# Layer norm with residual: three early loads moved from SyncE's DMA queue to ScalarE's

## The chip, the cores and the metric

The kernel runs on one core of a Trainium2 chip. The metric is device time in microseconds (us), which includes some 1.3 us outside the profiled span. "Fast" is the undisturbed state (granted clock 1.0).

## The reference

```python
# x, residual: (16, 1024, 512) float32; gamma, beta: 512; eps 1e-5
z = x + residual
mean = np.mean(z, axis=-1, keepdims=True)
var = np.var(z, axis=-1, keepdims=True)
out = (gamma * (z - mean) / np.sqrt(var + eps) + beta).astype(np.float32)
```

That is 33.5 MB of x, 33.5 MB of residual and 33.5 MB of output: 100.7 MB that must cross the DMA engines (100.68 MB in the profile), and little arithmetic.

## The kernel before

A "row" below is one 512-vector in each of the 128 partitions, 0.262 MB; there are 128 rows of x, of residual and of output. `x16+16` in the plan is one DMA that loads rows 16 to 31 of x; `r` is the residual, `o` a store. SyncE issues all of them, in this order:

```python
BLOCK = 16; Z_ROWS = 64; R_ROWS = 32        # rows in the buffers zbuf and rbuf
PLAN = """
x0+8 r0+8 x8+8 r8+8 x16+16 r16+16 x32+16 r32+16
x48+16 r48+16 o0+16 r64+16 x64+16 o16+16 r80+16 x80+16
... o64+16 o80+16 o96+16 o112+12 o124+4
"""
ADDS = [4, 4, 8] * 7 + [4] * 4              # rows of GpSimd's adds, in order
EARLY = 2                                   # the first two loads go ahead of the opening barrier

for k, src in enumerate((gamma, beta)):     # 2 KB each, on ScalarE's queue
    nc.scalar.dma_start(out=gb_row[:, k * D : (k + 1) * D], in_=src[None, :]).then_inc(s_gb[k], 16)
...
def move(out, in_, s):
    i = nc.sync.dma_start(out=out, in_=in_).then_inc(s, 16)
    if len(first) < EARLY:
        first.append(i.ins)                 # moved ahead of the barrier at the end of the build
...
    elif kind == "r":
        wait_rows(s_add, "add", lo + n - R_ROWS)   # rbuf holds 32 rows: r32 waits for 16 added rows
        move(part(rbuf, R_ROWS, lo, n), dram(rf, lo, n), sr[loads_r.index((lo, n))])
```

GpSimd (POOL in the profile) adds x and residual as both land. ScalarE (ACT) makes the sums, VectorE (DVE) normalizes in place, SyncE stores. TensorE spreads gamma and beta over the partitions once, in the opening.

## Time and profile before

| | us |
|---|---|
| median, first 3 runs | 238.73 (238.37 to 238.76) |
| span of the profiled run | 236.9 |
| ACT busy, DVE busy, POOL busy | 185.5, 177.2, 143.0 |

The page of the kernel before: the span in 40 slices of 5.9 us with the busy share of the DMA engines in tenths and the rate, then the DMA queues (packets, MB, share of 16 engines' time), then the chain of work that ended last, by engine.

```profile
DMA  8999999999999999999999999999999999999996
GB/s 310 443 432 426 426 443 443 443 443 443 426 415 398 443 443 443 426 420 409 431 437 443 443 443 432 420 407 429 443 437 437 409 432 448 437 420 437 426 430 285
q1 hardware_dynamic: 4176, 100.67, 99.2%
q10 hardware_dynamic: 4, 0.00, 0.0%
DMA 71%; POOL 9%; ACT 9%; DVE 2%; issue 2%; SPq 1%; ACTq 0%; DVEq 0%; POOLq 0%
```

Queue q1 is SyncE's ring, q10 ScalarE's; a ring is the queue of transfers that one issuing engine hands to the DMA engines. (A slice of the GB/s line counts whole packets of 16 or 32 KB, so it goes in steps of about 5.5, 32 KB in 5.92 us, and can show more than the engines keep up: 443 here, where 16 packets of 32 KB in 1213 ns are 432.) One ring alone keeps all 16 DMA engines busy for 99.2% of the span, in every slice but the two ends. The DMA engines bound this kernel; no compute engine is busy more than 78%.

The timeline of the kernel before, in its opening: start us, length us, engine, line, operation, operands; in brackets what an idle engine waited for. SPq and ACTq are the sequencers of SyncE and ScalarE, issuing DMAs.

```profile
0.00 0.38 SPq L146 DMA_DIRECT2D zbuf<-in_x_dram  x1
0.43 0.42 SPq L146 DMA_DIRECT2D rbuf<-in_residual_dram  x1
1.91 0.33 SPq L146 DMA_DIRECT2D zbuf<-in_x_dram  x1
1.92 0.52 ACTq L124 DMA_DIRECT2D gb_row<-in_gamma_dram  x1
...
12.33 8.95 POOL L180 TENSOR_TENSOR zbuf<-zbuf,rbuf 128x2048 f32<-128x2048 f32 x2 [11.90 <-DMA rbuf<-in_residual_dram]
22.12 8.87 POOL L180 TENSOR_TENSOR zbuf<-zbuf,rbuf 128x4096 f32<-128x4096 f32 x1 [0.83 <-DMA rbuf<-in_residual_dram]
41.55 17.83 POOL L180 TENSOR_TENSOR zbuf<-zbuf,rbuf 128x2048 f32<-128x2048 f32 x3 [10.56 <-DMA rbuf<-in_residual_dram]
...
59.41 0.33 SPq L146 DMA_DIRECT2D rbuf<-in_residual_dram  x1
```

The last line is the issue of r48, which must wait until 32 rows are added (until 59.39 us). By then the ring still holds work until x48 lands at 70.53 us. The packet records of the trace add what the page does not print: the first packets start at 1.01 us, a 16 KB packet takes 611 ns and a 32 KB packet 1213 ns at the median, one after the other on each engine, and the 16 engines are idle for 1.17 us on average up to 20 us and for about 0.06 us in all from there to 220 us. (Idle time here is the mean over 16 engines of the time without a packet of 512 bytes or more.)

### The profile page before, as it was taken

To read this page: it belongs to the slowest core of one execution; us is meant where nothing else is said; L and a number is where in the kernel's file an instruction comes from. 1 tells how busy PE (TensorE), PEld (TensorE's weight loads), DVE (VectorE), ACT (ScalarE), POOL (GpSimd) and SP (SyncE) were. 2 spreads that over 40 slices of the span, in tenths; PEclk is the share of its full clock that TensorE was granted. 3 is DMA by queue.
4 is the path that set the end of the run, shared out by engine and by line. 5 is a ranking of instruction groups with operands and counts; after the bars stand their busy time and mean duration, and the time that the engine had idled before them with its cause. 6 is when DMAs were issued, how large, how long until landed. Compare 5 with 4: busy or idle time off the path is not lost.

```text
span 236.9 us, 1471 instructions
## 1 busy us (share of the span) xinstructions
PE 3.7 (2%) x4; PEld 1.2 (0%) x4; DVE 177.2 (75%) x290; ACT 185.5 (78%) x545; POOL 143.0 (60%) x29
## 2 busy tenths in 40 slices
PE   0600000000000000000000000000000000000000
PEld 0100000000000000000000000000000000000000
DVE  0001977939699999999898989896989895698920
ACT  2019879497999999999999998979998956999300
POOL 0098920999799699604995059944995049950000
DMA  8999999999999999999999999999999999999996
GB/s 310 443 432 426 426 443 443 443 443 443 426 415 398 443 443 443 426 420 409 431 437 443 443 443 432 420 407 429 443 437 437 409 432 448 437 420 437 426 430 285
DMA packets 4181, 100.68 MB, mean 425 GB/s; under 512 B 466, under 2 KB 466, under 8 KB 468
## 3 DMA queue, kind: packets, MB, share of 16 engines
q1 hardware_dynamic: 4176, 100.67, 99.2%
q14 instruction: 1, 0.01, 0.0%
q10 hardware_dynamic: 4, 0.00, 0.0%
HBM read 67.11 MB, written 33.55 MB: 425 GB/s over the span
## 4 chain that ended last, share of the span: by engine, by line
DMA 71%; POOL 9%; ACT 9%; DVE 2%; issue 2%; SPq 1%; ACTq 0%; DVEq 0%; POOLq 0%
DMA out_dram<-zbuf 49%; DMA rbuf<-in_residual_dram 16%; POOL zbuf L180 9%; DMA zbuf<-in_x_dram 6%; ACT junk_s L212 5%; ACT junk_m L202 4%; SPq L146 1%; DVE zbuf L240 1%; DVE zbuf L252 1%; ACTq L202 0%; DVEq L240 0%; ACT std L221 0%; DVE rstd L249 0%; ACTq L193 0%; POOLq L177 0%
## 5 line engine op out<-in xcount | busy, mean ns | idle before, releaser
L180 POOL TENSOR_TENSOR zbuf<-zbuf,rbuf 128x2048 f32<-128x2048 f32 (+1 forms) x25 | 142.8, 5740 | 67.6 <-DMA zbuf<-in_x_dram 40.8
L240 DVE SCALAR_TENSOR_TENSOR zbuf<-zbuf,nm,gamma_p 128x512 f32 x128 | 87.1, 743 | 46.3 <-ACT junk_s L212 46.3
L202 ACT ACTIVATE junk_m<-zbuf 128x512 f32 x128 | 74.9, 585 | 29.1 <-POOL zbuf L180 27.5
L212 ACT ACTIVATE junk_s<-zbuf,nm 128x512 f32 x128 | 88.8, 694 | 1.0
L252 DVE SCALAR_TENSOR_TENSOR zbuf<-zbuf,rstd,beta_p 128x512 f32 x128 | 87.1, 743 | 1.1
L212 ACT ACTIVATION_READ_ACCUMULATOR junk_s<-zbuf,nm 128x1 f32 x128 | 23.9, 187 | 0.0
L202 ACT ACTIVATION_READ_ACCUMULATOR junk_m<-zbuf 128x1 f32 x128 | 23.9, 187 | 0.0
L221 ACT ACTIVATE std<-ssq,eps_t 128x4 f32<-128x4 f32 x32 | 9.5, 297 | 3.0
L249 DVE RECIPROCAL rstd<-std 128x4 f32<-128x4 f32 x32 | 5.5, 170 | 0.0
L190 ACT ACT_TABLE_LOAD x1 | 1.3, 1283 | 2.7 <-PEq L60 2.7
L132 PE MATMUL gamma_p<-gb_row,ones 1*128 1x512 f32 x2 | 2.0, 1119 | 7.2 <-DMA gb_row<-in_gamma_dram 7.2
L132 PE MATMUL beta_p<-gb_row,ones 1*128 1x512 f32 x2 | 1.9, 1052 | 0.0
L127 DVE MEMSET ones<- 1x128 f32 x1 | 0.2, 165 | 2.0 <-PEq L60 2.0
L132 PEld LDWEIGHTS beta_p<-gb_row,ones 1*128 1x128 f32 x2 | 0.7, 328 | 1.0 <-issue 0.5
L132 PEld LDWEIGHTS gamma_p<-gb_row,ones 1*128 1x128 f32 x2 | 0.5, 308 | 7.1 <-issue 7.1
L288 POOL MEMSET const-float32-0.0<- 128x1 f32 x1 | 0.1, 98 | 0.2 <-issue 0.2
L288 POOL MEMSET const-bfloat16-1.0<- 128x1 bf16 x1 | 0.1, 101 | 0.0
L288 POOL MEMSET const-uint8-127<- 128x1 uint8 x1 | 0.1, 101 | 0.0
L288 POOL MEMSET const-float32-1.0<- 128x1 f32 x1 | 0.1, 98 | 0.0
L128 DVE MEMSET eps_t<- 128x1 f32 x1 | 0.1, 59 | 0.0
## 6 DMA issues: line engine op xcount, KB each, us to landing
rbuf<-in_residual_dram SPq DMA_DIRECT2D x7, 4096.0 KB, 30.5
out_dram<-zbuf SPq DMA_DIRECT2D x7, 4096.0 KB, 28.6
zbuf<-in_x_dram SPq DMA_DIRECT2D x5, 4096.0 KB, 28.9
zbuf<-in_x_dram SPq DMA_DIRECT2D x6, 2048.0 KB, 14.9
rbuf<-in_residual_dram SPq DMA_DIRECT2D x2, 2048.0 KB, 15.7
out_dram<-zbuf SPq DMA_DIRECT2D x1, 3072.0 KB, 13.5
out_dram<-zbuf SPq DMA_DIRECT2D x1, 1024.0 KB, 10.2
gb_row<-in_gamma_dram ACTq DMA_DIRECT2D x1, 2.0 KB
```

Source lines behind the costliest of these rows:

```text
L127: nc.vector.memset(ones[:, :], 1.0).then_inc(s_const, 1)
L132: nc.tensor.matmul(dest[:, :], ones[:, :], gb_row[:, k * D : (k + 1) * D], start=True, stop=True).then_inc(s_pe, 1)
L146: i = nc.sync.dma_start(out=out, in_=in_).then_inc(s, 16)
L180: nc.gpsimd.tensor_tensor(out=z, in0=z, in1=part(rbuf, R_ROWS, lo, n), op=ALU.add).then_inc(s_add, n)
L190: act.preload_act_table_set("sqrt_and_others")
L202: i = act.activation(out=junk_m[k][:, :], in_=zk[k], func=ACT.Identity, scale=-inv_d, accum_out=nm[j][:, k : k + 1],)
L212: i = act.activation(out=junk_s[k][:, :], in_=zk[k], func=ACT.Square, bias=nm[j][:, k : k + 1], accum_out=ssq[j][:, k : k + 1],)
L221: act.activation(out=std[j][:, :], in_=ssq[j][:, :], func=ACT.Sqrt, bias=eps_t[:, 0:1], scale=inv_d,).then_inc(s_std, TURN)
L240: dve.scalar_tensor_tensor(out=zk[k], in0=zk[k], scalar=nm[j][:, k : k + 1], in1=gamma_p[:, :], op0=ALU.add, op1=ALU.mult,)
L249: dve.reciprocal(out=rstd[j][:, :], in_=std[j][:, :]).then_inc(s_dve, TURN)
L252: i = dve.scalar_tensor_tensor(out=zk[k], in0=zk[k], scalar=rstd[j][:, k : k + 1], in1=beta_p[:, :], op0=ALU.mult, op1=ALU.add,)
L288: nc = _bacc.Bacc("TRN2", target_bir_lowering=False, num_devices=1)
```

## The change

The intent is that two rings feed the DMA engines in the opening, instead of one sequencer that issues load after load.

```diff
-    def move(out, in_, s):
-        i = nc.sync.dma_start(out=out, in_=in_).then_inc(s, 16)
+    def move(out, in_, s, eng=nc.sync):
+        i = eng.dma_start(out=out, in_=in_).then_inc(s, 16)
 ...
             wait_rows(s_add, "add", lo + n - R_ROWS)
-            move(part(rbuf, R_ROWS, lo, n), dram(rf, lo, n), sr[loads_r.index((lo, n))])
+            eng = nc.scalar if lo + n <= R_ROWS else nc.sync
+            move(part(rbuf, R_ROWS, lo, n), dram(rf, lo, n), sr[loads_r.index((lo, n))], eng)
```

ScalarE now issues r0 ahead of the barrier, then gamma, beta, r8 and r16. SyncE issues x0, x8, x16, x32 and all the rest.

## The prediction

> **What bounds the kernel now.** The DMA engines. The table of DMA queues has q1 (SyncE's ring) busy for 99.2% of 16 engines' span of 236.9 us, for 100.67 MB. A 16 KB packet takes 611 ns at its median, a 32 KB packet 1213 ns, back to back: 16 x 16384 B / 611 ns = 429 GB/s. [...] 100.68 MB at 429 to 432 GB/s is 233 to 235 us (estimate from those packets); 2 to 4 us are left for both ends. ACT is busy 78%.

> **The opening.** In the timeline SyncE issues x0 at 0.00 and r0 at 0.43 us, then x8 to x32 from 1.91 to 4.26 us, 0.33 to 0.49 us each. The first packets start at 1.0 us and take 1.1 to 1.5 us; from 2.3 us the engines never run dry: x0 alone is 8 packets of 611 ns per engine, 4.9 us. A second ring has no gap to fill; 1.0 us before the first packet and some 0.6 us of its latency are idle, but x0's issue, unchanged, sets these.

> **What moves.** r0, r8 and r16 go to ScalarE's queue: r0 before the opening barrier, r8 and r16 behind gamma and beta. ScalarE gets three issues of 0.4 us; its table load (1.28 us, from 2.71 us) comes 0.5 to 1 us later. Its first activation waits for POOL until 17.06 us: free.

> **Order of landing.** [...] No run shows it yet. If it holds, x0 lands near 12 us instead of 7.3, with r0 still near 12.2; x8 and r8 near 22 (were 17.1 and 22.0); x16 and r16 near 41 (were 31.7 and 41.4). Adds need both inputs, so the first, third and fourth start as now (12.33, 22.12, 41.55 us). Gamma and beta fall in behind r0 and land near 12 us instead of 7; PE ends near 15 us, and DVE first needs them at 22.77 us: free. r32 is still issued at 31.0 us behind the third add, r48 at 59.4 us, while the ring's work lasts to 70.5 us (landing of x48): 11 us of slack. Nothing reaches steady state or tail.

> **Time.** Bytes, packet times and ends are unchanged: I predict 238.6 us, 8 in 10 within 237.7 to 240.0. Faster by over 2%: 0.01. Within 2%: 0.95. Slower by over 2%: 0.04.

> **What would show it.** Queues: q1 loses 8.4 MB (32 of 384 rows of 0.26 MB) to q10; their shares still sum to about 99%. x0 and r0 land within 1 us of each other near 12 us; x16 and r16 near 41. POOL's first adds start within 0.5 us of before. PE moves by 5 us; DVE's loop does not. The rate over the span is 424 to 427 GB/s. Wrong if the GB/s of slices 2 to 7 drop, or adds start over 1 us later.

> **What would make it wrong.** (1) Switching rings costs time per packet: 1% of 39 us is 0.4 us, 10% would be 4 us. (2) Engines share unequally: with SyncE's ring favoured, x32 overtakes r16 and delays the fourth add; beyond 11 us the DMA queue runs dry. [...]

Cut where marked: a figure for the DMA rate, a rule for how an engine shares two rings, and a third risk. "It" in "If it holds" is that rule, so the landings there were the author's estimate; what the trace shows of them comes below. The sum: 233 to 235 us for the bytes, from the packet times, and 2 to 4 us for both ends, 235 to 239 in all, and the 238.6 predicted is the measured time before, with nothing added.

## The result, and the profile after

The changed kernel takes 238.62 us at the median (238.19 to 239.56, 6 runs), the kernel before 238.64 us (238.37 to 238.76, 6 runs). Ratios in this document are the mean time of one kernel's fast runs over that of the other's of the same rounds, so not quite the ratio of the medians: here 1.0006, with a 95% interval from 0.9984 to 1.0028.

The page of the changed kernel, the same lines:

```profile
DMA  8999999999999999999999999999999999999995
GB/s 309 438 430 449 435 415 441 435 441 441 430 441 435 369 441 441 435 441 441 424 430 424 419 424 435 441 410 430 460 435 430 397 438 432 435 441 424 420 449 222
q1 hardware_dynamic: 3744, 92.28, 90.7%
q10 hardware_dynamic: 436, 8.39, 8.2%
DMA 50%; ACT 28%; POOL 9%; issue 4%; DVE 2%; ACTq 2%; SPq 0%; DVEq 0%; POOLq 0%
```

The 8.39 MB have moved to q10, and the two shares sum to 98.9%. The first slice moved 309 GB/s (310 before): the opening gained nothing. The first packet starts at 1.01 us, as before, and the engines are idle for 1.19 us up to 20 us (1.17 before). There was no hole for a second ring to fill.

The chain, however, reads differently: ACT has 28% of it instead of 9%. (In late_two_rings, the same two rings issued later, it has 56%: the size of this share differs, its direction does not.) The timeline of the changed kernel shows where this begins:

```profile
0.00 2.94 SPq L146 DMA_DIRECT2D zbuf<-in_x_dram  x4
0.12 0.38 ACTq L146 DMA_DIRECT2D rbuf<-in_residual_dram  x1
1.58 0.50 ACTq L124 DMA_DIRECT2D gb_row<-in_gamma_dram  x1
2.37 0.95 ACTq L146 DMA_DIRECT2D rbuf<-in_residual_dram  x2
...
13.16 8.95 POOL L181 TENSOR_TENSOR zbuf<-zbuf,rbuf 128x2048 f32<-128x2048 f32 x2 [12.73 <-DMA rbuf<-in_residual_dram]
28.09 8.87 POOL L181 TENSOR_TENSOR zbuf<-zbuf,rbuf 128x4096 f32<-128x4096 f32 x1 [5.97 <-DMA rbuf<-in_residual_dram]
47.52 17.83 POOL L181 TENSOR_TENSOR zbuf<-zbuf,rbuf 128x2048 f32<-128x2048 f32 x3 [10.57 <-DMA rbuf<-in_residual_dram]
...
65.37 0.33 SPq L146 DMA_DIRECT2D rbuf<-in_residual_dram  x1
```

All issues were done sooner, and yet the third add (second POOL line) starts 5.97 us later than before, the fourth also 5.97 us later, and r48 is issued 5.96 us later. The brackets name the residual. The landings, which are the first and the last of the 16 semaphore updates of a load (one for each DMA engine), show why:

| load | before: first, last engine | changed: first, last engine |
|---|---|---|
| x0 | 7.00, 7.29 | 11.07, 11.78 |
| r0 | 11.87, 12.17 | 12.31, 13.00 |
| x8 | 16.76, 17.08 | 18.79, 21.56 |
| r8 | 21.66, 21.96 | 22.69, 27.93 |
| x16 | 31.38, 31.68 | 35.26, 40.49 |
| r16 | 41.09, 41.39 | 42.12, 47.36 |
| x32 | 50.80, 51.10 | 50.63, 51.43 |
| gamma | 7.03 | 13.81 |

By x32 the same bytes have landed at the same time. In between, r8 and r16 are about 1 us late on the first engine and 5 to 6 us late on the last one: a single engine lags.

The packet records have no engine number. But on one engine a packet starts where the last one ended (to within 18 ns for 99% of the data packets, while both rings work in the changed kernel), so that 16 streams can be put together. This is the engine with the gamma and beta packets, beside an ordinary engine, in the changed kernel from 10.9 us on (start us: ring:bytes; the 4-byte packets are semaphore updates):

```
with gamma and beta
10.92 q1:4      10.92 q10:16384  11.53 q1:16384  12.14 q10:4      12.14 q1:16384
12.75 q10:2048  12.83 q1:16384   13.44 q10:4     13.44 q1:16384   14.05 q10:2048
14.13 q1:16384  14.74 q10:4      14.74 q1:16384  15.35 q10:16384  15.96 q1:16384
... 18.39 q1:4  18.39 q10:16384  19.00 q1:32768  20.21 q10:16384  20.82 q1:32768
22.03 q10:16384 22.63 q1:32768   23.84 q10:16384 24.45 q1:32768   25.66 q10:16384
26.27 q1:32768  27.48 q10:4 (r8 has landed)
ordinary
10.86 q1:4      10.86 q10:16384  11.47 q1:16384  12.08 q10:4      12.08 q1:16384
12.69 q10:16384 13.30 q1:16384   13.90 q10:16384 14.51 q1:16384   15.12 q10:16384
... 19.97 q10:16384 20.58 q1:4      20.58 q10:16384 21.19 q1:32768
22.40 q10:4 (r8 has landed)
```

In this trace the rings take strict turns, one packet each. From the first r0 packet to the last of r16, on all 16 engines, 644 of 726 pairs of successive data packets change rings; the other 82 are the places of 4-byte packets, five on each engine and two more here. A 4-byte packet, 9 ns long, uses a whole turn, and the other ring answers it with 16 KB, 611 ns. Gamma, beta and their two semaphore updates cost the residual ring four turns on this engine. Its last four r8 packets and their semaphore update therefore each wait for a packet of x16, which is of 32 KB (1213 ns), so that SyncE's ring gets twice the bytes per turn. What the first four turns cost is 4 x 0.61 = 2.4 us; the larger packets of the other ring about double it.

The ordinary engine shows where the other 1 us comes from. Its last data packet of r8 ends at 21.19 us; on 15 engines these ends lie between 21.04 and 21.76 us, where they lay between 21.23 and 21.54 before. The data is therefore not later there. But the semaphore update, which tells GpSimd that the load has landed, must wait for its own turn behind one 32 KB packet of x16, 1.21 us, while in the kernel before it followed the data at once.

This is the explanation read from the trace. The experiments test it, and ask why 6 us of lateness cost nothing.

### The profile page after: what moved, and what is told of

The parts are those of the page before. It is cut to its first block, busy times and chain, and to the rows that moved or that the text cites. A ratio compares the mean times of both kernels' runs of the same rounds, so it can differ in the third digit from the quotient of the medians.

```text
span 237.9 us, 1471 instructions
## 1 busy us (share of the span) xinstructions
PE 3.7 (2%) x4; PEld 1.1 (0%) x4; DVE 177.3 (75%) x290; ACT 185.6 (78%) x545; POOL 142.9 (60%) x29
## 2 busy tenths in 40 slices
DMA packets 4181, 100.68 MB, mean 423 GB/s; under 512 B 466, under 2 KB 466, under 8 KB 468
## 3 DMA queue, kind: packets, MB, share of 16 engines
q1 hardware_dynamic: 3744, 92.28, 90.7%
q10 hardware_dynamic: 436, 8.39, 8.2%
## 4 chain that ended last, share of the span: by engine, by line
DMA 50%; ACT 28%; POOL 9%; issue 4%; DVE 2%; ACTq 2%; SPq 0%; DVEq 0%; POOLq 0%
DMA out_dram<-zbuf 23%; DMA rbuf<-in_residual_dram 19%; ACT junk_s L213 16%; ACT junk_m L203 12%; POOL zbuf L181 9%; DMA zbuf<-in_x_dram 8%; DVE zbuf L241 1%; DVE zbuf L253 1%; ACTq L203 1%; ACTq L124 0%; SPq L146 0%; ACT std L222 0%; ACTq L194 0%; ACTq L146 0%; ACTq L200 0%
```

## The experiments

Three sets, each on one chip. "Before" is each time the kernel before in the same rounds. All outputs were correct.

| kernel | median us | before us | ratio, 95% interval | third, fourth add start |
|---|---|---|---|---|
| gb_pool | 238.39 | 238.44 | 0.9996 (0.9977 to 1.0014) | 23.34, 42.76 |
| gb_sync | 238.43 | 238.44 | 1.0004 (0.9984 to 1.0024) | 24.31, 42.72 |
| even_packets | 238.77 | 238.44 | 1.0019 (0.9999 to 1.0039) | 24.96, 34.74 |
| gb_in_eight | 243.11 | 238.44 | 1.0193 (1.0174 to 1.0212) | 41.60, 51.29 |
| r16_after_x32 | 240.70 | 238.48 | 1.0094 (1.0069 to 1.0120) | 22.39, 51.52 |
| r16_after_x48 | 250.52 | 238.48 | 1.0510 (1.0478 to 1.0542) | 22.13, 60.99 |
| late_one_ring | 239.88 | 238.48 | 1.0059 (1.0042 to 1.0075) | 23.45, 42.88 |
| late_two_rings | 239.80 | 238.48 | 1.0067 (1.0037 to 1.0096) | 30.77, 50.18 |
| after_again | 238.50 | 238.37 | 1.0013 (0.9994 to 1.0032) | 27.92, 47.34 |
| gb_pool_again | 238.24 | 238.37 | 0.9992 (0.9977 to 1.0007) | 23.51, 42.93 |
| before_again | 238.22 | 238.37 | 0.9996 (0.9980 to 1.0012) | 22.13, 41.55 |

(In even_packets, the fourth add has other rows ready sooner, see there.) For r16_after_x32 and the late pair the interval excludes 1.

### gb_pool: is it gamma and beta?

In the changed kernel:

```diff
-        nc.scalar.dma_start(out=gb_row[:, k * D : (k + 1) * D], in_=src[None, :]).then_inc(
+        nc.gpsimd.dma_start(out=gb_row[:, k * D : (k + 1) * D], in_=src[None, :]).then_inc(
```

> The changed kernel with gamma and beta issued by GpSimd, so that ScalarE's ring holds residual loads alone. Theory (turns by packet: in the changed kernel the two 2 KB packets and their two semaphore packets cost the residual ring four turns on one DMA engine): r8's last engine lands at 22.7 to 23.3 us instead of 27.9, r16's at 42.3 to 43.0 instead of 47.4, so the third add starts near 23.2 (28.1 in the changed kernel) and the fourth near 42.8 (47.5). Rival (ScalarE's ring is served worse by itself): r8 still near 28. Time: the theory that late adds only eat slack says 238.6 us, as before. The rival that the second ring won time in the opening and lost it again to the late adds says below 238.0 here.

The timeline of gb_pool, the adds:

```profile
23.34 8.87 POOL L181 TENSOR_TENSOR zbuf<-zbuf,rbuf 128x4096 f32<-128x4096 f32 x1 [1.44 <-DMA rbuf<-in_residual_dram]
42.76 17.82 POOL L181 TENSOR_TENSOR zbuf<-zbuf,rbuf 128x2048 f32<-128x2048 f32 x3 [10.55 <-DMA rbuf<-in_residual_dram]
```

r8 landed from 22.77 to 23.18 us on all engines, r16 at 42.60. The 5 us lag of one engine is gone with the tiny loads. (GpSimd's ring carried them as 32 packets of 128 bytes, spread over the engines, with 32 updates (q0 in its page, 64 packets), and was done by 11 us, before r8's first packet; so this run moved them in time too.) The 1 us lag of all engines stays: r8's data has ended by 21.56 us on every engine, as before the change, and its update again waits 1.21 us behind a packet of x16. SyncE's ring had two packets through on each engine before the first packet of ScalarE's ring (from 2.8 us on), so r ends behind its x, and the next x stands in front of r's update. The time is that of the kernel before. So the late adds did not hide a gain of the second ring, or none above 0.23% (the lower end of the interval).

### gb_sync: is ScalarE's ring served worse?

```diff
-        nc.scalar.dma_start(out=gb_row[:, k * D : (k + 1) * D], in_=src[None, :]).then_inc(
+        nc.sync.dma_start(out=gb_row[:, k * D : (k + 1) * D], in_=src[None, :]).then_inc(
```

> The changed kernel with gamma and beta issued by SyncE, between x0 and x8: the mirror image. Theory of turns: now x8's last engine lands late, near 27, and x16's near 46, while r8 lands by 22.5; the third add again starts near 27 to 28 us. Rival (ScalarE's ring is served worse): x8 near 21.6 as in the changed kernel and r8 near 28 or better, with the lag still on r. Time 238.6 us by slack.

The timeline of gb_sync, the third add:

```profile
24.31 8.87 POOL L181 TENSOR_TENSOR zbuf<-zbuf,rbuf 128x4096 f32<-128x4096 f32 x1 [2.44 <-DMA zbuf<-in_x_dram]
```

The bracket now names x instead of the residual: the lag went to the ring that holds the tiny packets. x8's last engine landed at 24.19 us, against 21.35 in gb_pool; r8 at 23.14. So the direction was right and the rival fell. The size was not: 27 was expected for x8, 46 for x16 and 27 to 28 for the third add, and 24.19, 41.18 and 24.31 were measured. The packets of that engine show two reasons. SyncE's ring starts ahead, which pays for part of the loss. And ScalarE's ring is empty on that engine from 38.3 us, so that x16 catches up alone; in the changed kernel the lagging r16 had x32 as its rival to the end.

### even_packets: does the packet size of the other ring count?

In the changed kernel, the plan's opening:

```diff
-x0+8 r0+8 x8+8 r8+8 x16+16 r16+16 x32+16 r32+16
+x0+8 r0+8 x8+8 r8+8 x16+8 r16+8 x24+8 r24+8 x32+16 r32+16
```

> The changed kernel with the 16-row loads of rows 16 to 31 split in two, so that all packets of both rings in the opening are of 16 KB. Theory: four lost turns now cost 4 x 0.61 = 2.4 us instead of some 5 us, so r8 lands near 24.7 us (27.9 in the changed kernel), r16's first half near 34.5, its second near 44.5; the third add starts near 24.9 and the fourth near 34.7. If packet size had no part, r8 stays near 27.5. Time 238.6 us.

The timeline of even_packets, the third and fourth add:

```profile
24.96 8.88 POOL L181 TENSOR_TENSOR zbuf<-zbuf,rbuf 128x4096 f32<-128x4096 f32 x1 [3.02 <-DMA rbuf<-in_residual_dram]
34.74 8.98 POOL L181 TENSOR_TENSOR zbuf<-zbuf,rbuf 128x2048 f32<-128x2048 f32 x2 [0.91 <-DMA rbuf<-in_residual_dram]
```

Measured: r8 at 24.80 us, the first half of r16 at 34.58, the third add at 24.96, the fourth at 34.74. The lag of the slowest engine behind the first one on r8 is 2.65 us (22.15 to 24.80), against 5.24 us in the changed kernel: with equal packets four turns cost about 4 x 0.61 us. On the ordinary engines r8's update now waits 0.61 us instead of 1.21. The one miss is the second half, r24: 47.39 instead of 44.5. It runs beside x32, whose packets are still of 32 KB, so its lag grows to 5.0 us, by the same rule.

### gb_in_eight: more turns, and how much lateness is free?

In the changed kernel, gamma and beta in four pieces of 512 bytes each (and the wait for them at 64 instead of 16):

```diff
-        nc.scalar.dma_start(out=gb_row[:, k * D : (k + 1) * D], in_=src[None, :]).then_inc(
-            s_gb[k], 16
-        )
+        for q in range(4):
+            w = D // 4
+            nc.scalar.dma_start(
+                out=gb_row[:, k * D + q * w : k * D + (q + 1) * w],
+                in_=src[None, q * w : (q + 1) * w],
+            ).then_inc(s_gb[k], 16)
```

> The changed kernel with gamma and beta loaded in four pieces each, 16 tiny packets in front of r8 on one DMA engine instead of 4. Theory of turns: on that engine r8 lands near 41 us and r16 near 51, when the other ring has run out of loads, so the third add starts near 41.5 (28.1) and the fourth near 51.3 (47.5). Time: slack still covers it, r32 is issued at 50.4 just as the rings empty at 51: 238.6 to 240 us. Rival (late adds cost time one for one): about 238.6 + 4 us or more.

The timeline of gb_in_eight, the adds and the issue of r32:

```profile
41.60 8.80 POOL L184 TENSOR_TENSOR zbuf<-zbuf,rbuf 128x4096 f32<-128x4096 f32 x1 [19.64 <-DMA rbuf<-in_residual_dram]
51.29 53.42 POOL L184 TENSOR_TENSOR zbuf<-zbuf,rbuf 128x2048 f32<-128x2048 f32 x9 [0.89 <-DMA rbuf<-in_residual_dram]
50.43 0.33 SPq L149 DMA_DIRECT2D rbuf<-in_residual_dram  x1
```

The turns were counted right: 16 tiny packets in place of 4 put r8 at 41.44 us (41 expected) and the adds at 41.60 and 51.29 (41.5 and 51.3). Four kilobytes, cut small enough, hold up a 2 MB load by 18 us (41.44 against 23.18 us in gb_pool). The time was counted wrong: 243.11 us, 4.7 above before, where up to 240 was expected. The rival ("late adds cost time one for one") named 242.6 us or more, which the measured time fits; but one for one does not hold either: here the third add was 19.5 us late and the fourth 9.7, while in r16_after_x32 (below) 9.97 us of lateness cost only 2.2 us. There are two holes. The DMA engines went dry from 50.3 to about 52 us, since r32 was issued at 50.43 us, too near the end of the queued work. And near 228 us they went dry again, because ScalarE had never caught up. Windows of ScalarE's work at the end of the span (start:end, length, ACT busy (instructions), clock, DMA share, GB/s), first of the kernel before:

```profile
220.00:245.00 25.00, 1.23 (x5) 1.00 0.59 253
```

then of the changed kernel:

```profile
220.00:245.00 25.00, 3.02 (x9) 1.00 0.61 261
```

and of gb_in_eight:

```profile
220.00:245.00 25.00, 10.78 (x32) 1.00 0.70 298
```

ScalarE finishes its last rows later and later, and the store of rows 112 to 123 behind it is issued at 220.88, 222.66 and 230.57 us. In the first two the engines have stores queued until about 225.5 us; in gb_in_eight they run out from 227.5 us on and wait until 231.5, 3.4 us of idle time per engine. So there is a second reserve, ScalarE's idle time, which the prediction did not count. In the kernel before ScalarE waited 27.5 us in all for adds, 13.1 of it for the first one; in gb_in_eight it waits for two adds only, and then runs behind without a pause.

### r16_after_x32 and r16_after_x48: the size of the slack, with one ring

In the kernel before:

```diff
-x0+8 r0+8 x8+8 r8+8 x16+16 r16+16 x32+16 r32+16
+x0+8 r0+8 x8+8 r8+8 x16+16 x32+16 r16+16 r32+16
```

```diff
-x0+8 r0+8 x8+8 r8+8 x16+16 r16+16 x32+16 r32+16
-x48+16 r48+16 o0+16 r64+16 x64+16 o16+16 r80+16 x80+16
+x0+8 r0+8 x8+8 r8+8 x16+16 x32+16 x48+16 r16+16
+r32+16 r48+16 o0+16 r64+16 x64+16 o16+16 r80+16 x80+16
```

> The kernel before, one ring, with r16 issued behind x32: r16 lands near 51.1 us instead of 41.4, the fourth add starts near 51.3, r48 is issued near 69.1 instead of 59.4, against the ring's end near 70.5. By the slack of 11 us read from the profile the time stays 238.6 us (within 0.5). If late adds cost time one for one, it is about 248.

> The kernel before, one ring, with r16 issued behind x32 and x48: r16 lands near 60.8 us, r48 is issued near 78.8, but the ring runs dry near 70.5 and gets no packet until about 79.8. This overdraws the slack by about 9 us: 247.5 us (range 245.5 to 249), with a hole of about 9 us in the DMA slices near 70 to 80 us. If adds had unlimited slack, 238.6.

Both adds fell where expected (51.52 and 60.99 us), and both times were above expectation: 240.70 and 250.52 us. The timeline of r16_after_x32 around the issue of r48:

```profile
69.31 0.33 SPq L146 DMA_DIRECT2D rbuf<-in_residual_dram  x1
69.68 0.43 SPq L146 DMA_DIRECT2D out_dram<-zbuf  x1
```

Its engines ran dry from 69.7 us on, before x48's semaphore was complete at 70.80; the first packet of r48 came at 70.27, 1.0 us after its issue; and these first packets of 32 KB took 1.3 to 2.3 us instead of 1.21. r48 landed 11.9 us behind x48, where it had been 10.0. The windows of r16_after_x48 show the large hole:

```profile
66.00:70.00 4.00, 0.00 (x0) 0.00 (x0) 0.00 (x0) 3.97 (x13) 4.00 (x2) 1.00 0.90 385
70.00:75.00 5.00, 0.00 (x0) 0.00 (x0) 3.54 (x7) 4.88 (x16) 5.00 (x1) 1.00 0.00 0
75.00:80.00 5.00, 0.00 (x0) 0.00 (x0) 4.77 (x9) 3.40 (x10) 5.00 (x2) 1.00 0.27 72
```

(The last three columns are the clock, the DMA share and GB/s.) The DMA rate is zero from 70 to 75 us.

From the two: the fourth add was 9.97 us late (51.52 - 41.55) and the time rose by 2.22; it was 19.44 us late and the time rose by 12.04. Late minus paid is 7.75 and 7.40 us. If every us beyond the slack costs one us, the free lateness of this add is about 7.5 us. But if the slow first packets (1.3 to 2.3 us instead of 1.21) are paid once, however long the hole, which these runs do not settle, the slack is larger: in r16_after_x32 the engines ran dry at 69.7 us and the first packet of r48 started 1.0 us after its issue, so that an issue of r48 up to 68.7 us, 9.3 us later than in the kernel before, would leave no hole (an estimate from these times). What the runs show is that 7.3 us are free (the late pair below) and 9.97 us are not; no run lies between. The 11 us that the prediction took from "r48 issued at 59.4, x48 landed at 70.5" are too many in either case. The lateness of the changed kernel, 5.97 us, lies inside, with at least 1.3 us to spare.

### late_one_ring and late_two_rings: what the opening does depend on

In the kernel before, and likewise in the changed kernel:

```diff
-EARLY = 2
+EARLY = 0
```

> The kernel before with no load issued ahead of the opening barrier. If the first issue sets the opening, the first packet starts 1.2 to 1.9 us later against the start of the program and the time is 239.8 to 240.5 us.

> The changed kernel with no load issued ahead of the opening barrier, so that the two sequencers issue x0 and r0 in parallel behind it, and gamma and beta stand in front of r0. If the second ring saves nothing but issue time that nobody waits for, this equals the one-ring kernel of the same form within 0.3 us (239.8 to 240.5). If a second ring helps where little is queued at the start, it is 0.4 us or more below that kernel. By the theory of turns gamma's four turns now fall before r0, so r0 lags by up to 2.4 us on one engine and r8 by about 5 us.

The timeline of late_one_ring, then of late_two_rings:

```profile
1.39 0.38 SPq L146 DMA_DIRECT2D zbuf<-in_x_dram  x1
1.82 0.42 SPq L146 DMA_DIRECT2D rbuf<-in_residual_dram  x1
```

```profile
1.39 1.98 SPq L146 DMA_DIRECT2D zbuf<-in_x_dram  x4
2.21 1.56 ACTq L146 DMA_DIRECT2D rbuf<-in_residual_dram  x3
```

With x0 issued 1.39 us later, the first packet of x0 is at 2.40 us in both, and the medians rise by 1.40 and 1.32 us: the first issue is worth its full time, and the number of rings nothing that shows (0.08 us between the medians). The lag in late_two_rings is larger than expected, and on all engines: r0's first engine landed at 15.62 us. In the packets, on 15 of the 16 engines five or six packets of x0 pass before the first of r0, which starts between 6.1 and 6.9 us, though r0 was issued only 0.82 us behind x0. In the changed kernel, with 0.12 us between the issues, it was two. Why, the profile does not show. The fourth add starts at 50.18 us, 7.3 us later than in late_one_ring, whose opening is the same; the engines had no hole (DMA share 0.97 from 66 to 70 us, 1.08 to 75) and the time is the same (239.80 and 239.88 us), so that these 7.3 us were free.

### after_again, gb_pool_again, before_again: the small differences

No edits; the changed kernel, gb_pool and the kernel before, with five rounds.

> The changed kernel once more, with more rounds. Slack theory: within 0.2% of the kernel before. If the lag of 5 to 6 us on r8 and r16 costs something at the end, it shows as 0.1 to 0.3% above both of the other kernels of this set. The profile: DMA engines idle for about 1.2 us at the start, none in between, and the ends of the 16 engines spread over 1.5 to 2.5 us, as in the kernel before.

> The changed kernel with gamma and beta issued by GpSimd, with more rounds: two rings without the lag. Slack theory: the same time as the kernel before and as the changed kernel, 238.3 to 238.6 us. If two rings gain anything in the opening that the lag hides, it is at least 0.1% below the kernel before.

> The kernel before against itself, to size the noise: ratio 1.000 within 0.1%. Its profile shows how far the time of the last engine's last packet moves between executions of one program: if the 1.0 us by which the changed kernel's profiled span was longer is such noise, spans of this kernel spread by as much, or its last packet ends anywhere from 236 to 237.5 us.

All three intervals contain 1. The first profile of the changed kernel had a span of 237.9 us, 1.0 longer than before: the first DMA engine was done at nearly the same time (235.32 us, 235.24 before), the last one at 237.88 instead of 236.89; its repeat had 237.0, and its runs went from 238.19 to 239.56 us. This is spread between executions of one program. The kernel before spread from 238.08 to 239.01 us in this set, so the changed kernel's larger spread is not established. Nor is a gain of gb_pool, 0.08% below before with an interval across zero. A cost of the lag near 0.1%, as in 1.0013 and in even_packets' 1.0019, can neither be shown nor excluded. No version here beats the kernel before.

## Why the prediction was right, and where it was not

- **"A second ring has no gap to fill": right, and shown.** Engine idle time up to 20 us is 1.17 us before and 1.19 after, the first packet starts at 1.01 us in both, and gb_pool, two rings without the lag, is at 0.9996 and 0.9992. The late pair shows that x0's issue sets the opening (1.39 us later, 1.40 and 1.32 us longer).
- **The time: right.** 238.6 predicted, 238.62 measured.
- **Queues: right; rate: just outside.** 8.39 MB moved to q10; shares of 90.7% and 8.2%. The rate over the span was 423 GB/s (424 to 427 predicted) in a profile that fell on a longer execution, and 425 in its repeat (100.68 MB in 237.0 us).
- **"x0 and r0 land within 1 us": nearly.** 11.78 and 13.00 us; the head start of SyncE's ring, and the turn that r0's update waits, were not foreseen.
- **"Adds start as now": wrong.** The first was 0.83 us late, the third and fourth 5.97. The prediction had named "adds start over 1 us later" as a sign of error, and it occurred. The step that failed is "x8 and r8 near 22 ... x16 and r16 near 41". It gives the two rings equal shares by bytes, where the trace shows turns by packet (16 KB against 32 KB from 19.0 us on, on the engine shown). The prediction saw gamma and beta fall in behind r0, but not that each of their packets and semaphore updates costs the ring a turn, nor that turns of 16 KB would alternate with turns of 32 KB, nor that an update waits a turn even without them (1.21 us on the ordinary engines). gb_pool, gb_sync, even_packets and gb_in_eight show each part.
- **Gamma near 12 us, PE done near 15: 13.81 and near 17.7.** The same lost turns. It was free, as predicted: DVE's first work in the loop starts at 23.60 us, behind ACT.
- **"11 us of slack": mis-sized; between 7.3 and 9.97 us by experiment.** The landing of a load is later than the moment when its engines run dry (70.80 against 69.7 us for x48 in r16_after_x32), and the restart there took 1.0 us to the first packet plus up to 1.1 us more for it. "Nothing reaches steady state or tail" was wrong too: the lateness reaches the last stores through ScalarE (220.88 to 222.66 us), and cost nothing that shows, because stores were still queued until about 225.5 us.

The time was right because the DMA engines were not idle between the opening and the end (0.08 us from 20 to 220 us in the changed kernel, 0.06 before), and because the error in the order of landing was smaller than the slack. The first was predicted. The second is in part luck: the prediction foresaw neither the 6 us of lateness nor the true slack. With 16 tiny packets instead of 4 (gb_in_eight) the same turns cost 4.7 us.
